# Later use of modulation weights and pinned first activations in a two-layer diffusion trunk on one Trainium2 core

## The chip, the cores and the metric

The kernel runs on one core of a Trainium2 chip. The metric is device microseconds for one execution of the whole program, as the median of several runs. The engines are PE (TensorE, with its weight loads as PEld), DVE (VectorE), ACT (ScalarE), POOL (GpSimd) and SP (SyncE), whose queue issues most of the DMAs; ACT's queue issues the rest. Each engine works through its own instructions in the order in which they stand in its program.

## What is computed

The reference is one step of a two-layer trunk with 512 latent tokens and 128 context tokens, model width 1024, all in float32. Layer 0 mixes tokens with neighbourhood attention, layer 1 with grouped-query attention. Each is followed by a gated feed-forward block with a depthwise convolution of width 3. Every sub-layer is normed before and after, and scaled, shifted and gated by rows of a modulation vector. Cut to what matters here:

```python
sh_as, sc_as, g_as, sh_fs, sc_fs, g_fs = adaln(c, ada_w[l], ada_b[l])   # silu(c) @ (1024 x 6144) + b
...
u = h @ w_up                                   # 1024 -> 2 x 2816
u = conv3(u) * conv_w + conv_b                 # along the tokens
a, gt = jnp.split(u, 2, axis=-1)
y = (jax.nn.silu(a) * gt) @ w_down             # 2816 -> 1024
x = x + g_fs * rmsnorm(y, norm_ffn_post[l])
```

## The kernel before

**Split products.** A float32 operand is held as a rounded high part and the low rest (`wh`/`wl`, `ahi`/`alo`, `vh`/`vl`, `ah`/`al`). ACT casts the high part (L165 for weights read whole, L1107 for up-projection blocks, L1075 for activations), DVE or POOL subtracts it to get the low part (L167, L1108, L1077). A product is then three matmuls per 128 rows.

**The up-projection.** The 5632 output columns are 22 pairs of blocks, one value block and one gate block of 128 columns each; a pair is called p. The first two pairs (`PLAIN`) run as plain products; the other 20 use a seven-product scheme in which sums of weight blocks (DVE, L1128 to L1131) meet sums of activation blocks. Inside the loop over p the seven products come in the order 6, 5, 1 (of the next pair), 7, 2 (of the next pair), 3, 4, each of 12 matmuls of 322 columns, into three banks `ux`, `uy`, `uz`. After each product its result is evicted: `c`, `u` and `v` are copies on ACT (L1161), `C` are sums on DVE (L1203, L1210, L1212) or a copy on ACT (L1216). A complete `C` goes through the convolution: `t` on ACT (L1182), two taps on DVE (L1184), then `sl` on ACT and `act` on DVE, and SP stores `act` of that pair to DRAM (L1223). `fetch` (L1099) loads the weights of later pairs into four buffers.

**Modulation weights.** `ada_work` is a generator. Each step of the loop of products calls `next(ada)` once. It loads 128x1024 pieces of `ada_w` (tile `wr`, three buffers, L275), uses three at a time in small matmuls (`ada`, L114), adds a bias (`arow`, L297) and writes a row of modulation values to DRAM (`modrow`, from ACT's queue). Layer 0's up-projection carries 48 such pieces (six rows of the next steps), layer 1's carries 8. The first layer's attention stage also calls it with steps = 1.

**The down-projection.** `load_dn(k, c0, c1)` loads one 128-row block of `w_down` (L163 in a helper) and the activations of pair k from DRAM (`ain`, three buffers, L1073), casts them to `ahi` (ACT, L1075, four buffers) and subtracts to `alo` (DVE, L1077). Two of these calls are written inside the last pair of the up-projection, the others after it. The token columns are handled in two ranges, 0 to 383 first (c0 = 0).

**The end of the mixer.** `Mix.second` runs the second half of the output projection tile by tile. During tile t it issues `fin.turns(t - 2)` (transposes to PSUM `tr`, ACT copies), `fin.residual(t - 1)` (DVE L377 and L386, ACT L348), and `low()`, which is the DVE subtraction of the low part of the transposed tile (`B<-tr,B`, L220). The first product of the up-projection reads that low part.

**What sets the order.** PE's order is exactly as written: a helper chains each matmul to the one before. On the other engines and on SP's queue a scheduler picks at build time, from what has its inputs and a free buffer, so an instruction may stand far ahead of the place where it was written. `tc.keep_in_program_order` holds an instruction to its written place. In the kernel before the scheduler put the first seven loads of `ain`, and the first four casts `ahi` and subtractions `alo`, into the first pairs of the up-projection, since `act` of pair k exists soon after pair k.

## Time and profile before

| | |
|---|---|
| median of 3 runs | 1622.42 us (1619.99 to 1624.73) |
| the profiled execution's own time | 1619.4 us |
| its span in the trace | 1617.6 us |
| mean granted TensorE clock | 0.984 |
| busy: PE, DVE, ACT, POOL | 1540.5, 1028.2, 860.7, 723.6 us |
| layer 0 up-projection (seven-product part) | about 427 to 705 us |
| layer 1 up-projection (seven-product part) | about 1198 to 1460 us |

The trace is one execution. A row of the timeline has start, duration, engine, line, operation, tiles, count and, in brackets, how long the engine sat idle before it and what ended that. Rows of the table of waits have the waiting instruction, what released it, the sum, the number and the longest.

### The profile page before, as it was taken

Reading aid. Unit: us, or ns where it says so; the run is one execution under the profiler, and the core shown is the slowest. Engines: PE = TensorE matmul, PEld = TensorE weight load, DVE = VectorE, ACT = ScalarE, POOL = GpSimd, SP = SyncE. Lnnn points to the kernel's source line nnn. Section 1 sums busy time; section 2 is a strip of 40 time slices with the busy share of each in tenths; the row PEclk is TensorE's granted clock in tenths of the full one; section 3 lists DMA queues with packets and bytes.
Section 4 is the critical chain, followed back from the end, with each engine's and each line's share of the span. In section 5 each row is a group of like instructions: output and inputs, shape, how many; then the busy total and the mean of one; then the engine's idle time right before and its main releaser. Section 6 shows DMA issues by size and latency. Waiting matters only on the chain.

```text
span 1617.6 us, 26048 instructions
## 1 busy us (share of the span) xinstructions
PE 1540.5 (95%) x9709; PEld 1357.0 (84%) x9709; DVE 1028.2 (64%) x1646; ACT 860.7 (53%) x1641; POOL 723.6 (45%) x613
## 2 busy tenths in 40 slices
PE   5999999899999999999999898999999999999998
PEld 3889899778988999998887667778889899998886
DVE  3453533539787666865656867774887887875554
ACT  3474655545555555654453536764555666564433
POOL 1554554324335555534444344441424556562433
PEclk8999999999999999999999998999999999999999
DMA  9745454236467764368574110004644333338664
GB/s 288 185 111 145 118 149 117 61 118 195 144 217 243 233 214 150 112 206 296 170 240 135 59 40 14 2 1 157 195 134 142 118 103 112 115 115 283 208 208 141
DMA packets 193211, 242.42 MB, mean 150 GB/s; under 512 B 11100, under 2 KB 149564, under 8 KB 193084
## 3 DMA queue, kind: packets, MB, share of 16 engines
q1 hardware_dynamic: 182224, 233.13, 45.2%
q10 hardware_dynamic: 10860, 7.62, 2.7%
q8 instruction: 76, 1.25, 0.3%
q14 instruction: 51, 0.42, 0.1%
HBM read 214.38 MB, written 26.34 MB: 149 GB/s over the span
## 4 chain that ended last, share of the span: by engine, by line
PE 65%; DVE 11%; POOL 8%; issue 6%; DMA 5%; ACT 3%; SPq 1%; ACTq 1%; POOLq 0%; DVEq 0%
PE acc L114 18%; PE ux L114 11%; PE y L114 7%; PE qk L114 5%; PE uz L114 4%; PE po L114 4%; PE s L114 3%; PE uy L114 3%; PE vp L114 3%; PE tp L117 3%; POOL wl L1108 3%; PE ada L114 2%; POOL vl L1108 2%; DMA wr<-in_ada_w 2%; DVE t L1184 1%
## 5 line engine op out<-in xcount | busy, mean ns | idle before, releaser
L167 POOL TENSOR_TENSOR wl<-wr,wh 128x1024 fp32r<-128x1024 f32 x74 | 181.3, 2453 | 257.9 <-ACT wh L165 249.8
L1108 POOL TENSOR_TENSOR wl<-wr,wh 128x1024 fp32r<-128x1024 f32 x80 | 193.9, 2446 | 36.9 <-ACT wh L1107 29.9
L114 PE MATMUL ux<-B,wh 128*128 128x322 f32 x832 | 201.2, 313 | 2.2 <-DVE B L220 1.6
L1184 DVE SCALAR_TENSOR_TENSOR t<-C,cw,t 128x644 f32<-128x644 f32 x176 | 156.3, 888 | 51.8 <-ACT t L1182 51.2
L114 PE MATMUL acc<-wh,alo 128*128 128x512 f32 x440 | 172.0, 391 | 0.0
L114 PE MATMUL acc<-wh,ahi 128*128 128x512 f32 x440 | 171.9, 391 | 0.0
L114 PE MATMUL acc<-wl,ahi 128*128 128x512 f32 x440 | 171.8, 390 | 0.0
L165 ACT CAST wh<-wr 128x1024 fp32r<-128x1024 f32 x140 | 145.4, 1048 | 37.5 <-DMA wr<-in_ffn_w_down 26.8
L114 PE MATMUL uz<-B,wh 128*128 128x322 f32 x640 | 156.5, 312 | 1.4 <-ACT v L1161 1.4
L114 PEld LDWEIGHTS ux<-B,wh 128*128 128x128 f32 x832 | 144.0, 189 | 5.5 <-DVE B L220 2.2
L1077 DVE TENSOR_TENSOR alo<-ain,ahi 128x384 fp32r<-128x384 f32 (+1 forms) x88 | 79.0, 910 | 92.7 <-ACT ahi L1075 92.3
L114 PE MATMUL ux<-B,wl 128*128 128x322 f32 x416 | 129.3, 311 | 0.0
L114 PE MATMUL qk<-hT,wh 128*128 128x384 f32 (+1 forms) x512 | 123.0, 317 | 0.1
L1108 POOL TENSOR_TENSOR vl<-wr,vh 128x1024 fp32r<-128x1024 f32 x38 | 99.5, 2619 | 40.8 <-ACT vh L1107 40.6
L114 PEld LDWEIGHTS uz<-B,wh 128*128 128x128 f32 x640 | 110.9, 188 | 4.1 <-ACT v L1161 1.6
L1107 ACT CAST wh<-wr 128x1024 fp32r<-128x1024 f32 x88 | 88.8, 1049 | 36.2 <-DVE wr L1131 34.8
L1075 ACT CAST ahi<-ain 128x384 fp32r<-128x384 f32 (+1 forms) x88 | 40.1, 460 | 120.6 <-PE acc L114 90.5
L167 DVE TENSOR_TENSOR wl<-wr,wh 128x1024 fp32r<-128x1024 f32 x66 | 84.8, 1297 | 26.5 <-ACT wh L165 26.0
L1182 ACT ACTIVATE t<-C,cw 128x644 f32<-128x644 f32 x88 | 78.6, 893 | 42.5 <-DVE C L1212 35.7
L114 PE MATMUL uz<-B,wl 128*128 128x322 f32 x320 | 99.5, 311 | 0.0
L114 PEld LDWEIGHTS acc<-wl,ahi 128*128 128x128 f32 x440 | 82.6, 188 | 17.9
L114 PEld LDWEIGHTS acc<-wh,alo 128*128 128x128 f32 x440 | 82.6, 188 | 17.8
(249 smaller groups left out, 4008.9 us busy)
## 6 DMA issues: line engine op xcount, KB each, us to landing
wr<-in_ffn_w_up SPq DMA_DIRECT2D x88, 512.0 KB
wr<-in_ffn_w_down SPq DMA_DIRECT2D x88, 512.0 KB
wr<-in_ada_w SPq DMA_DIRECT2D x80, 512.0 KB
act<-act SPq DMA_DIRECT2D x44, 321.0 KB
wr<-in_na_w_qkv SPq DMA_DIRECT2D x24, 512.0 KB
mod<-modrow SPq DMA_DIRECT2D x20, 512.0 KB
ain<-act SPq DMA_DIRECT2D x44, 192.0 KB
wf<-in_ada_w SPq DMA_DIRECT2D x16, 512.0 KB
```

What stands on the lines that cost most here:

```text
L114: pe(nc.tensor.matmul(*a, **k))
L117: pe(nc.tensor.transpose(*a, **k))
L165: i = nc.scalar.copy(hi, raw)
L167: j = (low or nc.vector).tensor_sub(lo, raw, f32(hi))
L1075: nc.scalar.copy(hi[:, 0 : c1 - c0], ain[:, 0 : c1 - c0])
L1077: nc.vector.tensor_sub(lo[:, 0 : c1 - c0], ain[:, 0 : c1 - c0], f32(hi[:, 0 : c1 - c0]))
L1107: nc.scalar.copy(hl[0], src)
L1108: low.tensor_sub(hl[1], src, f32(hl[0]))
L1182: nc.scalar.activation(t, taps(0), AF.Identity, bias=cw[:, 3, n : n + 1], scale=cw[:, 1, n : n + 1])
L1184: nc.vector.scalar_tensor_tensor(t, taps(d), cw[:, w, n : n + 1], t, op0=ALU.mult, op1=ALU.add)
```

## The change

It has three parts. (1) In the two up-projections the generator of modulation weights yields four times, not once, between its first three loads and their use, and a group is used every eight products instead of six; the three loads of the next group are written in the first three of the eight steps. For steps = 1 nothing changes. (2) In `Mix.second`, for the last tile alone, `low()` is written before `fin.residual(t - 1)` instead of behind it. (3) For k < 4 of the first token range, the load `ain`, the cast `ahi` and the subtraction `alo` are held in program order.

```diff
-    def ada_work(p, rawp, group, steps, todo):
+    def ada_work(p, rawp, group, steps, todo, wait=1):
...
         for _ in range(group):
             load()
-        yield
+        for _ in range(wait):
+            yield
         while raws:
...
             for i in range(steps):
-                for _ in range(n * i // steps, n * (i + 1) // steps):
+                for _ in range(n if steps == 1 else i < n):
                     load()
                 yield
...
                         low = fin.turns(t - 2) if t >= 2 else None
+                        if low and t == NT - 1:
+                            low()
                         if t >= 1:
                             fin.residual(t - 1)
-                        if low:
+                        if low and t < NT - 1:
                             low()
...
         def load_dn(k, c0, c1, own=None):
+            pin = tc.keep_in_program_order if k < 4 and c0 == 0 else lambda i: i
...
-            nc.sync.dma_start(ain[:, 0 : c1 - c0], actd[k][:, c0:c1])
+            pin(nc.sync.dma_start(ain[:, 0 : c1 - c0], actd[k][:, c0:c1]))
...
-            nc.scalar.copy(hi[:, 0 : c1 - c0], ain[:, 0 : c1 - c0])
+            pin(nc.scalar.copy(hi[:, 0 : c1 - c0], ain[:, 0 : c1 - c0]))
...
-            nc.vector.tensor_sub(lo[:, 0 : c1 - c0], ain[:, 0 : c1 - c0], f32(hi[:, 0 : c1 - c0]))
+            pin(nc.vector.tensor_sub(lo[:, 0 : c1 - c0], ain[:, 0 : c1 - c0], f32(hi[:, 0 : c1 - c0])))
...
-                ada = ada_work(adap, s2.enter_context(pool("adar", 3, side)), 3, 6, todo)
+                ada = ada_work(adap, s2.enter_context(pool("adar", 3, side)), 3, 8, todo, 4)
```

Layer 0's 48 pieces make 16 groups of three: before, the last was used behind product 92 of 138, now behind 125. On PE the first group of a layer stands behind five products instead of two.

The first place is SP's queue at the start of layer 1's up-projection. `act_k` is the DRAM tensor of pair k, `wr<-in_ffn_w_up` the weights of later pairs. Before:

```order
L275 DMA wr<-in_ada_w 128x1024
L1073 DMA ain<-act_0_12441 128x384
L275 DMA wr<-in_ada_w 128x1024 x2
L1223 DMA act_1_12442<-act 128x642
L1073 DMA ain<-act_1_12442 128x384
L1099 DMA wr<-in_ffn_w_up 128x8x128 x2
L1223 DMA act_2_12443<-act 128x642
L1073 DMA ain<-act_2_12443 128x384
```

and after, from the store of pair 0:

```order
L1227 DMA act_0_12441<-act 128x642
L275 DMA wr<-in_ada_w 128x1024 x2
L1227 DMA act_1_12442<-act 128x642
L1103 DMA wr<-in_ffn_w_up 128x8x128 x2
L275 DMA wr<-in_ada_w 128x1024 x2
L1227 DMA act_2_12443<-act 128x642
```

The loads of `ain` are gone from this place; they stand in the last two pairs now.

The second place is ACT in the same pairs. Before:

```order
L1161 COPY u_13064<-ux 128x322
L1075 CAST ahi<-ain 128x384
L1161 COPY v_13091<-uz 128x322
L1182 ACTIVATE t<-C,cw_84 128x2x322
L1161 COPY c_13112<-ux 128x322
L1107 CAST wh<-wr 128x1024 x2
```

and after:

```order
L1165 COPY u_13064<-ux 128x322
L1165 COPY v_13079<-uz 128x322
L1165 COPY c_13098<-ux 128x322
L1186 ACTIVATE t<-C,cw_84 128x2x322
L1111 CAST wh<-wr 128x1024 x2
```

The cast of `ahi`, which stood between the eviction copies `u` and `v`, is no longer there.

The third place is ACT in the last two pairs of layer 1's up-projection, where the first casts for the down-projection (L165) stand. Before:

```order
L165 CAST wh<-wr 128x1024 x2
L1182 ACTIVATE t<-C,cw_84 128x2x322
L1216 COPY C<-ux 128x322
L1161 COPY u_15525<-ux 128x322
L1190 ACTIVATE sl<-t 128x644
L1182 ACTIVATE t<-C,cw_84 128x2x322
L1161 COPY v_15540<-uz 128x322
```

and after:

```order
L165 CAST wh<-wr 128x1024
L1079 CAST ahi<-ain 128x384
L165 CAST wh<-wr 128x1024
L1186 ACTIVATE t<-C,cw_84 128x2x322
L1220 COPY C<-ux 128x322
L1079 CAST ahi<-ain 128x384
L1165 COPY u_15525<-ux 128x322
L1194 ACTIVATE sl<-t 128x644
L1186 ACTIVATE t<-C,cw_84 128x2x322
L1165 COPY v_15540<-uz 128x322
```

Two casts of `ahi` stand now ahead of the copies `u` and `v` of the last pair, and two more behind them. On DVE the first `alo` stands there directly ahead of the sum `C<-uz` of the pair before.

## Prediction

> **What bounds the kernel now.** I read the page's first lines, then the busy time of the two up-projections, then PE's waits in each.

> ```profile
> span 1617.6 us, 26048 instructions
> PE 1540.5 (95%) x9709; PEld 1357.0 (84%) x9709; DVE 1028.2 (64%) x1646; ACT 860.7 (53%) x1641; POOL 723.6 (45%) x613
> ```

> PE is busy for 95% of the span. Its work is not changed by a single matmul, so the change can only win PE's idle time or lengthen it. The windows of layer 1's and layer 0's up-projections say how much there is (duration, then busy PE, PEld, DVE, ACT, POOL, granted clock, DMA share, GB/s):

> ```profile
> 1160.00:1460.00 300.00, 288.56 (x1953) 281.26 (x1952) 244.79 (x308) 177.21 (x261) 153.02 (x91) 1.00 0.40 126
> 395.00:705.00 310.00, 302.44 (x2228) 284.23 (x2227) 225.30 (x307) 172.95 (x254) 147.37 (x86) 0.99 0.57 185
> ```

> PE idles 7.6 us of layer 0's 310 and 11.4 us of layer 1's 300. DVE, the next busiest, has 82% in layer 1 and 73% in layer 0: near, not at the bound. What PE waited for, layer 0 first, then layer 1:

> ```profile
> PE ada L114 <- DMA wr<-in_ada_w: 4.0, 5, 1.6
> PE uy L114 <- DVE C L1232: 2.6, 1, 2.6
> PE ux L114 <- ACT u L1161: 0.5, 1, 0.5
> PE ux L114 <- POOL vl L1108: 0.4, 1, 0.4
> ```

> ```profile
> PE ada L114 <- DMA wr<-in_ada_w: 2.8, 3, 1.5
> PE uy L114 <- DVE C L1232: 2.6, 1, 2.6
> PE ux L114 <- POOL vl L1108: 1.6, 4, 0.7
> PE ux L114 <- DVE C L1210: 1.5, 1, 1.5
> PE uz L114 <- ACT v L1161: 1.4, 1, 1.4
> PE ux L114 <- DVE B L220: 0.8, 1, 0.8
> ```

> The first row of each is part 1 of the change; ACT `u`, ACT `v`, DVE `C` and some of POOL `vl` will turn out to be part 3; DVE `B L220` is part 2.

> **Part 1, the modulation weights.** PE at the first group of layer 0, a later group, and the queue's issue of that later group:

> ```profile
> 430.36 0.64 PE L114 MATMUL ada<-wr,scolp 128*32 128x256 f32 x8
> 432.61 0.64 PE L114 MATMUL ada<-wr,scolp 128*32 128x256 f32 x8 [1.61 <-DMA wr<-in_ada_w]
> 433.87 0.64 PE L114 MATMUL ada<-wr,scolp 128*32 128x256 f32 x8 [0.62 <-DMA wr<-in_ada_w]
> ...
> 497.28 0.64 PE L114 MATMUL ada<-wr,scolp 128*32 128x256 f32 x8 [0.59 <-DMA wr<-in_ada_w]
> ...
> 489.55 1.47 SPq L275 DMA_DIRECT2D wr<-in_ada_w  x3
> ```

> The first group finds its third piece 433.87 - 430.36 = 3.5 us late. It moves back by three products. A pair of seven products takes 12.46 us (row below), so a product is 1.78 us and the delay 5.3 us: enough. A later group is short by about 0.6 us on its third piece; the interval grows by two products, 3.6 us: also enough. So 4.0 + 2.8 = 6.8 us of shown waits go, eight of them. Each costs more than it shows, since the matmuls before and behind it no longer overlap; from the rows of part 3 I take 0.28 us for each, 2.2 us in all. Part 1: -9.0 us. The matmuls themselves stay. They now run to product 125 of 138, and the pieces come every eight products instead of six; PE fills that time anyway and the DMA engines were at 57% with the denser loads, so I cost the move at nothing. Without that cover it would cost a wait of some 0.6 us at a group again. On SP the loads still stand between stores of `act` and loads of `w_up`; ends for part 1 are 0, if the queue holds them back as long as before, and -9.0.

> **Part 3, where the casts leave.** The queue, ACT and PE at the second hoisted activation of layer 1, and two ACT casts `ah` of the undisturbed stretch:

> ```profile
> 1243.30 0.53 SPq L1223 DMA_DIRECT2D act<-act  x1
> 1248.78 0.32 SPq L1073 DMA_DIRECT2D ain<-act  x1
> ```

> ```profile
> 1243.79 0.62 ACT L1107 CAST ah<-wr 128x512 fp32r<-128x512 f32 x1 [0.36 <-PE ux L114]
> 1252.40 0.51 ACT L1075 CAST ahi<-ain 128x384 fp32r<-128x384 f32 x1 [6.41 <-DMA ain<-act]
> 1254.39 0.42 ACT L1161 COPY v<-uz 128x322 f32<-128x322 f32 x1
> 1260.53 0.62 ACT L1107 CAST ah<-wr 128x512 fp32r<-128x512 f32 x1 [0.43 <-PE ux L114]
> ...
> 1426.35 0.62 ACT L1107 CAST ah<-wr 128x512 fp32r<-128x512 f32 x1 [0.36 <-PE ux L114]
> 1438.81 0.62 ACT L1107 CAST ah<-wr 128x512 fp32r<-128x512 f32 x1 [0.36 <-PE ux L114]
> ```

> ```profile
> 1248.02 0.42 PE L114 MATMUL ux<-B,vl 128*128 128x322 f32 x1 [0.55 <-POOL vl L1108]
> ```

> SP issues `ain` only when the store of the same pair has landed, 5.5 us after that store. ACT then stands 6.41 us at `ahi`, and the copy `v` queued behind it is late; PE waits 1.4 us for `v` and 1.5 us for the `C` that needs it. A pair takes 1438.81 - 1426.35 = 12.46 us where nothing waits, this one 1260.53 - 1243.79 = 16.74: 4.28 us more, against shown waits of 0.55 + 1.4 + 1.5 = 3.4 in three places. That is the 0.28 us per wait used above. What goes: layer 1's `v` and `C` (2.9), the two longest of `vl` (0.55 and 0.7), layer 0's `u` (0.5): 4.65 us shown and 5 x 0.28: -6.1 us. The short rest of the `vl` waits I leave as it is.

> **Part 3, where the casts arrive.** The last two pairs of layer 1, on ACT, DVE, POOL, SP and PE; and a slow `alo` from before:

> ```profile
> 1448.01 1.04 ACT L165 CAST wh<-wr 128x1024 fp32r<-128x1024 f32 x1
> ...
> 1451.57 0.89 ACT L1182 ACTIVATE t<-C,cw 128x644 f32<-128x644 f32 x1 [0.57 <-DVE C L1212]
> ...
> 1455.92 0.42 ACT L1161 COPY v<-uz 128x322 f32<-128x322 f32 x1
> ```

> ```profile
> 1229.93 2.05 DVE L1077 TENSOR_TENSOR alo<-ain,ahi 128x384 fp32r<-128x384 f32 x1
> ...
> 1451.05 0.48 DVE L1212 TENSOR_TENSOR C<-uz,u 128x322 f32<-128x322 f32 x1
> ```

> ```profile
> 1447.23 5.77 POOL L1108 TENSOR_TENSOR wl<-wr,wh 128x1024 fp32r<-128x1024 f32 x2 [4.63 <-ACT wh L1107]
> ```

> ```profile
> 1437.45 2.69 SPq L163 DMA_DIRECT2D wr<-in_ffn_w_down  x2
> ```

> ```profile
> 1456.87 0.31 PE L114 MATMUL uz<-B,wh 128*128 128x322 f32 x1
> ```

> The first `alo` now stands ahead of `C<-uz` on DVE. ACT's `t` waits for that `C`, and `u`, `sl`, `t` and `v` are queued behind it. PE's product 3 accumulates in the bank that `v` copies, and starts at 1456.87, 0.53 us after `v` ends (1455.92 + 0.42). So a delay x costs x - 0.53 plus the 0.28. An `alo` of up to 0.53 us, about what its cast took on ACT (0.51), would cost nothing; beside a busy POOL it took 2.05 us, and POOL is in its two `wl` here. I take the latter: 1.8 us for each layer, +3.6 us; ends 0 and +3.6. The cast in ACT fits the idle time around it. `ain` for k = 0 is issued right behind the first `w_down`, so about 10 us before ACT reaches it (1437.45 to 1448.01); a lone load landed in 3.6 us (1248.78 to 1252.40). `ahi` for k = 2 and 3 is first needed behind the first two blocks of the down-projection, whose `w_down` casts are in time today.

> [...]

> **Part 2, the low half of the last tile.** DVE before the first product, and the two windows of the long wait, layer 0 and layer 1:

> ```profile
> 387.08 1.28 DVE L386 TENSOR_TENSOR xm<-xo,mod 128x512 f32<-128x512 f32 x2
> 388.29 0.76 DVE L220 TENSOR_TENSOR B<-tr,B 128x264 fp32r<-128x264 f32 x2
> ```

> ```profile
> 398.00:405.00 7.00, 4.43 (x20) 4.17 (x19) 6.93 (x10) 4.75 (x8) 0.15 (x4) 0.76 0.30 91
> 1171.00:1178.00 7.00, 4.43 (x30) 4.17 (x29) 7.00 (x10) 4.01 (x8) 0.13 (x2) 1.00 0.30 85
> ```

> One `B<-tr,B` passes one of the two L386, so PE's 0.8 us wait shrinks by some 0.6 us. But PE then waits 2.6 us for DVE's `C` L1232, and DVE is busy for all 7 us there; the same instructions in another order end at the same time. PE only arrives earlier at a longer wait: 0. Ends: -1.2 us for both layers if DVE follows, +1.7 us if the clock does (below).

> **Sum.** -9.0 - 6.1 + 3.6 + 0 = -11.5 us. The profiled execution took 1619.4 us, 3.0 below the median of the runs; taken from 1619.4 it gives 1607.9, from the median 1622.42 it gives 1610.9. I predict a median of 1611.

> **Rivals.** (a) The chain of DVE, ACT and POOL takes over in layer 1, so that PE's early gain is only waited away at `vl`. For it: DVE's 82%, and the four `vl` waits. Against: layer 0, where `ada` matmuls slow PE, shows a single one. It would take back part 1's share of layer 1, 2.8 + 3 x 0.28 = 3.6 us: 1614.5. (b) The loads stay late, since SP holds them behind stores: only part 3 is left, -2.5 us: 1619.9, no change. Against it: 489.55 to 497.28 is 7.7 us, and the need was 0.6 us. (c) Slower: the pinned casts wait for `ain` as they did before, now in the last pairs, where `w_down` is on the same queue. Each such wait costs 4.28 us by the pair above; with four of the eight the sum turns to +5.6 us, 1628, and from three on nothing is won. It needs a landing later than 10 us. (d) The clock: layer 0's window was granted 0.76, layer 1's 1.00, after the same 2.6 us wait. With PE's wait grown to 3.2 us, layer 1 could be halved too. A loss of 0.24 of 7 us is 1.7 us: 1612.6. [...]

> **How the numbers follow.** Forecast 0.58, (a) 0.16, (d) 0.10, (b) 0.10, (c) 0.06. About 0.3%, 4.9 us, is what a measurement of this kernel can tell from no change, so faster is below 1617.6: the forecast, (d) and most of (a), 0.81. Same: (b) and the slow end of (a), 0.13. Slower: 0.06. Range: low 1604, where the arrival costs nothing (-3.6) and DVE follows PE in part 2 or layer 0 keeps its clock (-1.2 to -1.7), rounded for the spread of the runs; high 1619, which leaves out (c) and most of (b).

> **What the profile after would show.** No PE wait for `in_ada_w` in either up-projection; if some stay, the lead is too short. No ACT wait for `ain` near the start; pairs of 12.46 us plus the `ada` matmuls there. PE waits of about 1.5 us at `uz` or `ux` in the last pair, on ACT `v` or `u`; none means the arrival was free. The waits at `B L220` shorter and those at `C L1232` longer by the same. Wrong would be: ACT waiting for `ain` in the last pairs, or `vl` waits that grow from 2.0 us by as much as the `ada` waits fall.

## The result, and the profile after

The changed kernel took 1611.22 us (1610.03 to 1611.9, four runs), the kernel before 1621.2 us beside it (1619.02 to 1624.73, four runs): ratio 0.9941, 95% interval 0.9922 to 0.9959. The forecast was 1611. The total came out; several of its terms did not, as the experiments show.

The page of the changed kernel, first lines:

```profile
span 1608.2 us, 26065 instructions
PE 1541.6 (96%) x9709; PEld 1360.4 (85%) x9709; DVE 1023.0 (64%) x1646; ACT 860.6 (54%) x1641; POOL 722.2 (45%) x613
```

PE does the same 9709 matmuls in 1541.6 us (1540.5 before); the span is 9.4 us shorter. What PE waits for after the change, layer 0 (395 to 705 us) and then layer 1 (1150 to 1460 us):

```profile
PE uy L114 <- DVE C L1236: 3.2, 1, 3.2
PE acc L114 <- DVE alo L1081: 0.2, 1, 0.2
```

```profile
PE uy L114 <- DVE C L1236: 3.2, 1, 3.2
PE ux L114 <- ACT u L1165: 0.9, 1, 0.9
PE ux L114 <- POOL vl L1112: 0.9, 4, 0.3
PE uz L114 <- ACT v L1165: 0.7, 1, 0.7
PE acc L114 <- DVE alo L1081: 0.3, 1, 0.3
PE ux L114 <- DVE B L220: 0.2, 1, 0.2
```

The rows for `in_ada_w` are gone from both layers (4.0 and 2.8 us before), and so are `u` in layer 0 and the waits of 1.4 us for `v` and 1.5 us for `C` in layer 1. New are `u` and `v` at the end of layer 1 and `alo` at the first product of the down-projection. `B L220` fell from 0.8 to 0.2, and the wait for `C` behind it rose from 2.6 to 3.2.

A pair of landmarks per layer measures the stretch between: PE's `uy` behind the long wait for `C`, and the first `acc`. Before, and after:

```profile
401.07 0.42 PE L114 MATMUL uy<-B,wh 128*128 128x322 f32 x1 [2.56 <-DVE C L1232]
705.31 0.39 PE L114 MATMUL acc<-wh,ahi 128*128 128x512 f32 x1
1173.96 0.41 PE L114 MATMUL uy<-B,wh 128*128 128x322 f32 x1 [2.57 <-DVE C L1232]
1460.42 0.40 PE L114 MATMUL acc<-wh,ahi 128*128 128x512 f32 x1
```

```profile
401.16 0.42 PE L114 MATMUL uy<-B,wh 128*128 128x322 f32 x1 [3.18 <-DVE C L1236]
698.74 0.40 PE L114 MATMUL acc<-wh,ahi 128*128 128x512 f32 x1
1168.51 0.42 PE L114 MATMUL uy<-B,wh 128*128 128x322 f32 x1 [3.18 <-DVE C L1236]
1450.43 0.40 PE L114 MATMUL acc<-wh,ahi 128*128 128x512 f32 x1
```

Layer 0 went from 705.31 - 401.07 = 304.24 to 297.58 us (-6.7), layer 1 from 286.46 to 281.92 us (-4.5). The prediction had about -4.4 and -7.1. Everything outside the two stretches grew by 1.8 us together, which gives the 9.4 us of the span; 0.6 of it lies behind layer 1's first `acc`, and the rest is not followed up here. Layer 1 lost part of its share at its start, where PE's granted clock was 0.50 behind the longer wait (windows of the changed kernel; the seventh value is the granted clock):

```profile
1166.40:1169.80 3.40, 1.29 (x8) 1.29 (x9) 3.40 (x5) 1.67 (x3) 0.13 (x2) 1.00 0.08 22
1169.80:1173.20 3.40, 3.40 (x15) 3.40 (x14) 3.40 (x6) 0.83 (x1) 0.00 (x0) 0.50 0.48 137
```

PE is busy for the whole 3.40 us of the second row at a granted clock of 0.50: by that share 1.7 us lost, an estimate. The profiled execution of the kernel before did not lose it here; it was granted 1.00 from 1169.58 to 1176.41 us, around the same wait.

### The profile page after: what moved, and what is told of

Same layout as the page of the kernel before. It is cut to its first block, busy times and chain, and to the rows that moved or that the text cites. A ratio compares the mean times of both kernels' runs of the same rounds, so it can differ in the third digit from the quotient of the medians.

```text
span 1608.2 us, 26065 instructions
## 1 busy us (share of the span) xinstructions
PE 1541.6 (96%) x9709; PEld 1360.4 (85%) x9709; DVE 1023.0 (64%) x1646; ACT 860.6 (54%) x1641; POOL 722.2 (45%) x613
## 4 chain that ended last, share of the span: by engine, by line
PE 73%; DVE 10%; POOL 6%; issue 4%; ACT 4%; DMA 2%; SPq 1%; ACTq 0%; POOLq 0%; DVEq 0%
PE acc L114 18%; PE ux L114 15%; PE y L114 7%; PE uz L114 6%; PE qk L114 5%; PE uy L114 4%; PE po L114 4%; PE s L114 4%; PE vp L114 3%; PE tp L117 3%; PE ada L114 2%; POOL wl L1112 1%; DVE al L1112 1%; POOL vl L1112 1%; DMA wf<-in_ada_w 1%
## 5 line engine op out<-in xcount | busy, mean ns | idle before, releaser
L114 PE MATMUL ux<-B,wh 128*128 128x322 f32 x832 | 201.9, 314 | 1.4 <-ACT u L1165 0.9
L114 PE MATMUL acc<-wh,alo 128*128 128x512 f32 x440 | 172.3, 392 | 0.6 <-DVE alo L1081 0.6
L114 PE MATMUL acc<-wh,ahi 128*128 128x512 f32 x440 | 171.9, 391 | 0.0
L114 PE MATMUL acc<-wl,ahi 128*128 128x512 f32 x440 | 171.9, 391 | 0.0
L165 ACT CAST wh<-wr 128x1024 fp32r<-128x1024 f32 x140 | 145.5, 1048 | 33.5 <-DMA wr<-in_ffn_w_down 24.3
L114 PE MATMUL uz<-B,wh 128*128 128x322 f32 x640 | 156.5, 313 | 0.7 <-ACT v L1165 0.7
L114 PEld LDWEIGHTS ux<-B,wh 128*128 128x128 f32 x832 | 145.0, 190 | 4.3 <-ACT u L1165 1.2
L114 PE MATMUL ux<-B,wl 128*128 128x322 f32 x416 | 130.1, 313 | 0.2
L114 PE MATMUL qk<-hT,wh 128*128 128x384 f32 (+1 forms) x512 | 122.8, 317 | 0.1
L114 PEld LDWEIGHTS uz<-B,wh 128*128 128x128 f32 x640 | 110.9, 188 | 3.6 <-ACT vh L1111 1.6
L114 PE MATMUL uz<-B,wl 128*128 128x322 f32 x320 | 99.5, 311 | 0.1
L114 PEld LDWEIGHTS acc<-wh,alo 128*128 128x128 f32 x440 | 82.5, 188 | 19.1 <-DVE alo L1081 1.4
L114 PEld LDWEIGHTS acc<-wl,ahi 128*128 128x128 f32 x440 | 82.6, 188 | 17.8
```

Source lines behind the costliest of these rows:

```text
L114: pe(nc.tensor.matmul(*a, **k))
L165: i = nc.scalar.copy(hi, raw)
```

## Experiments

Twelve kernels ran in three groups of four, each against the kernel before on the same chip. Times are medians; the difference to before is of medians in the same group. The ratio and its interval are not formed from these two medians and can differ from them: for the interval of eight alone the medians give -3.5 us, the ratio -1.9 us.

| kernel | time, us | against before, us | ratio (95%) |
|---|---|---|---|
| part 1 alone | 1606.53 | -14.2 | 0.9912 (0.9897 to 0.9926) |
| part 3 alone | 1620.08 | -0.6 | 0.9995 (0.9986 to 1.0004) |
| part 2 alone | 1621.16 | +0.5 | 1.0007 (0.9997 to 1.0018) |
| parts 1 and 3 | 1608.65 | -12.1 | 0.9918 (0.9905 to 0.9932) |
| before, one cast moved in layer 1 | 1617.54 | -2.1 | 0.9990 (0.9979 to 1.0001) |
| part 1, one cast moved in layer 0 | 1604.66 | -15.0 | 0.9914 (0.9899 to 0.9928) |
| lead of four alone | 1622.04 | +2.4 | 1.0021 (1.0011 to 1.0031) |
| interval of eight alone | 1616.10 | -3.5 | 0.9988 (0.9978 to 0.9998) |
| part 1 in layer 1 | 1610.70 | -9.1 | 0.9941 (0.9927 to 0.9955) |
| part 1 in layer 0 | 1614.59 | -5.2 | 0.9965 (0.9952 to 0.9979) |
| lead of four and part 3 | 1621.70 | +1.9 | 1.0005 (0.9994 to 1.0016) |
| parts 1 and 3, `alo` later | 1606.42 | -13.4 | 0.9915 (0.9901 to 0.9929) |

### Part 1 alone

```diff
-        yield
+        for _ in range(wait):
+            yield
...
-                for _ in range(n * i // steps, n * (i + 1) // steps):
+                for _ in range(n if steps == 1 else i < n):
...
-                ada = ada_work(adap, s2.enter_context(pool("adar", 3, side)), 3, 6, todo)
+                ada = ada_work(adap, s2.enter_context(pool("adar", 3, side)), 3, 8, todo, 4)
```

> The kernel before with part 1 alone (lead of four products, a group every eight, loads in the first three steps). Theory T, the terms of the prediction add up: the eight waits for in_ada_w go, -9.0 us, of which 5.4 in layer 0 (4.0 shown + 5 x 0.28) and 3.6 in layer 1 (2.8 + 3 x 0.28). Rival (a), the chain of DVE, ACT and POOL takes layer 1's share back: -5.4 us, and the PE waits at vl in layer 1 grow from 1.6 to some 4 us. Rival (b), the loads stay late on SP's queue: 0.

Measured: -14.2 us, beyond every theory. The same landmarks, and PE's waits in layer 1:

```profile
401.69 0.42 PE L114 MATMUL uy<-B,wh 128*128 128x322 f32 x1 [2.59 <-DVE C L1233]
700.46 0.39 PE L114 MATMUL acc<-wh,ahi 128*128 128x512 f32 x1
1168.08 0.41 PE L114 MATMUL uy<-B,wh 128*128 128x322 f32 x1 [2.58 <-DVE C L1233]
1447.54 0.40 PE L114 MATMUL acc<-wh,ahi 128*128 128x512 f32 x1
```

```profile
PE uy L114 <- DVE C L1233: 2.6, 1, 2.6
PE ux L114 <- POOL vl L1109: 2.2, 8, 0.6
PE ux L114 <- DVE B L220: 0.8, 1, 0.8
```

Layer 0 is 298.77 us long: -5.5, where -5.4 was expected. Layer 1 is 279.46: -7.0 instead of -3.6. The waits for `v` and `C` are gone there too, though the casts `ahi` are still in the early pairs. ACT at the fourth of them shows why:

```profile
1238.65 0.42 ACT L1162 COPY u<-ux 128x322 f32<-128x322 f32 x1
...
1240.38 0.43 ACT L1162 COPY v<-uz 128x322 f32<-128x322 f32 x1 [0.52 <-PE ux L114]
1240.70 0.52 ACT L1076 CAST ahi<-ain 128x384 fp32r<-128x384 f32 x1
```

In the kernel before this cast stood between `u` and `v` and held `v` up for 6.41 us of waiting; here the build-time order, chosen anew around the moved loads, has it behind `v`, with its input there. So what I had booked under part 3 was already won by part 1. The time fell by more than the two stretches, 14.2 against 12.5 us; the runs with part 1 in one layer take this up.

### Part 3 alone

```diff
+            pin = tc.keep_in_program_order if k < 4 and c0 == 0 else lambda i: i
...
+            pin(nc.sync.dma_start(ain[:, 0 : c1 - c0], actd[k][:, c0:c1]))
...
+            pin(nc.scalar.copy(hi[:, 0 : c1 - c0], ain[:, 0 : c1 - c0]))
...
+            pin(nc.vector.tensor_sub(lo[:, 0 : c1 - c0], ain[:, 0 : c1 - c0], f32(hi[:, 0 : c1 - c0])))
```

> The kernel before with part 3 alone (loads, casts and subtractions of the first four activations held in their written place). T: -6.1 us at the start of the two layers and +3.6 us at their ends, -2.5 us in all. If the arrival costs layer 1 alone, as the trace after suggests (waits of 0.95 and 0.72 for u and v in layer 1, none in layer 0, where the last group of modulation weights leaves PE behind): about -4 us. If it costs nothing: -6.1 us. Here layer 0 has no late group of weights before the last pair (its last stands behind product 92), so T expects the waits for u and v in layer 0 too, and the sum of -2.5.

Measured: no difference. The early waits went, and the late ones came in both layers (`u` 0.65 and `v` 0.74 in layer 0, 0.94 and 0.75 in layer 1, and 0.25 and 0.23 for `alo` a few us behind the first `acc`). But the first group of weights of layer 1 waits for 3.7 us here (2.8 before), and the clock follows:

```profile
1203.40:1206.80 3.40, 0.96 (x16) 0.32 (x16) 1.78 (x2) 3.34 (x5) 2.65 (x2) 1.00 0.86 293
1206.80:1210.20 3.40, 2.94 (x21) 1.63 (x14) 1.79 (x2) 0.18 (x1) 0.10 (x1) 0.50 1.00 308
1210.20:1213.60 3.40, 3.40 (x15) 3.40 (x14) 0.00 (x0) 0.43 (x1) 0.00 (x0) 0.50 0.86 242
```

PE idles for 2.44 us of the first window and is granted 0.50 in the next two, by that share a loss of up to 3.4 us. Layer 0's first group waited 3.0 us in this execution (2.2 before) and had a half clock of 3.4 us behind it too, another 1.7 us by the same estimate. Its two stretches are 1.3 and 1.0 us longer than those of before, though the early waits are gone. So the trace shows the early waits leaving, and it does not show what part 3 is worth by itself.

### Part 2 alone

```diff
+                        if low and t == NT - 1:
+                            low()
                         if t >= 1:
                             fin.residual(t - 1)
-                        if low:
+                        if low and t < NT - 1:
                             low()
```

> The kernel before with part 2 alone (low half of the last tile earlier). T: the wait at B L220 shrinks by 0.6 us in each layer and the wait at C L1232 grows by as much, from 2.57 to 3.18 us; 0 us. Rival (d), the longer wait halves the clock in layer 1 as in layer 0: +1.7 us, and layer 1's clock drops right behind that wait. If the change of the clock in layer 1 after was chance, layer 1 is not halved here.

Measured: no difference. `B L220` went to 0.2 and `C` to 3.2 us, as expected, but layer 1's clock stayed full behind that wait:

```profile
1168.80:1172.20 3.40, 1.87 (x13) 1.62 (x12) 2.31 (x5) 3.37 (x8) 1.89 (x4) 1.00 0.70 247
1172.20:1175.60 3.40, 1.74 (x12) 1.74 (x13) 3.40 (x6) 1.25 (x2) 0.13 (x2) 1.00 0.24 67
1175.60:1179.00 3.40, 3.40 (x26) 3.40 (x25) 3.40 (x6) 1.78 (x3) 0.00 (x0) 1.00 0.31 92
```

The wait ran from 1170.68 to 1173.87, so a boundary of the clock's windows (of 3.413 us, last section) split it into 1.5 and 1.7 us. In the changed kernel 2.15 us of a wait of the same length fell into one window, and the next was granted 0.50. So the longer wait alone did not bring a half clock here; the two executions differ in where it fell in the windows.

### Parts 1 and 3, without part 2

The changed kernel with the edit of part 2 undone.

> The changed kernel without part 2 (parts 1 and 3 on the kernel before). T with part 2 at zero: as the changed kernel, about -10 us against before. Rival (d), the 3.18 us wait is what halves layer 1's clock: this kernel keeps 2.57 us there, layer 1 stays at full clock, and it is 1.7 us faster than the changed kernel, about -12 us against before.

Measured: -12.1 us, layer 1 at full clock behind the wait of 2.57 us. Its layer 1 took 280.12 us, 1.8 less than in the changed kernel, about the 1.7 us estimated for its window at 0.50. As times, its ratio and that of the changed kernel overlap, so what part 2 costs there is shown by the two traces alone. Beside part 1 alone (same group) it is 2.1 us slower by the medians, with overlapping intervals: on top of part 1, part 3 gained nothing that can be measured.

### One cast moved

On the kernel before, and on part 1 alone, an order was added: `ahi` of each of the first four activations behind the copy `v` of its pair. In the built order this moves one cast and its `alo` in each kernel: in layer 1 of the one, in layer 0 of the other. In the first, SP also issues one load of `w_up` apart from its partner.

```diff
-            nc.scalar.copy(hi[:, 0 : c1 - c0], ain[:, 0 : c1 - c0])
+            i = nc.scalar.copy(hi[:, 0 : c1 - c0], ain[:, 0 : c1 - c0])
+            if k < 4 and c0 == 0:
+                tc.add_manual_dep(i.ins, vcopy[k + 2].ins.name, no_sync, reason="order")
...
-                nc.scalar.copy(small[name, p], u)
+                i = nc.scalar.copy(small[name, p], u)
+                if name == "v5":
+                    vcopy[p] = i
```

> The kernel before, and one thing moved: in layer 1 the fourth early cast ahi (and its subtraction alo) stands behind the copy v of its pair on ACT, instead of between u and v; the other seven early casts stay where they are, and so do the modulation weights. Theory P (what costs is the place among the eviction copies where the build-time order puts a late cast, not that the cast stands in the early pairs): the waits for v (1.36), for C (1.52) and most of the two vl waits around them go, the pair of 16.74 us becomes one of about 12.5 to 13, so -3.5 to -4.3 us. Theory Q (the early loads and casts themselves cost, through SP's queue, as part 3 assumes): the waits only move to c or to the next u, 0 to -1 us.

> Part 1 alone, and one thing moved: in layer 0 the fourth early cast ahi (and its alo) stands behind the copies u and v of its pair instead of ahead of u. Theory P: the one wait for u that part 1 alone still has there (1.14 us) goes, -1.1 to -1.4 us against part 1 alone, so about -15 us against before; no other wait appears. Theory Q: the wait turns up at c or v, no change against part 1 alone.

On the kernel before: -2.1 us by the medians, the interval just reaching no change. The trace is clearer. ACT at the moved cast:

```profile
1254.60 0.42 ACT L1164 COPY v<-uz 128x322 f32<-128x322 f32 x1
1256.19 0.52 ACT L1076 CAST ahi<-ain 128x384 fp32r<-128x384 f32 x1 [1.18 <-DMA ain<-act]
1256.61 0.42 ACT L1164 COPY c<-ux 128x322 f32<-128x322 f32 x1
```

The cast still waits for its input, and nobody waits for it: PE has no wait for `v` or `C` there, and the pair between two casts `ah` of ACT takes 12.47 (1248.62 to 1261.09) instead of 16.74 us. P holds for the waits, Q does not. The time of this execution does not show it: it is the longest of the twelve, its first group of layer 1 waited 4.1 us and the clock was then halved for 6.8 us, so its layer 1 takes 286.41 us, as before (286.46). That the median fell by 2.1 us and not by 3.5 or more is not explained by this one trace.

On part 1: 1604.66 us, the lowest median of all. The wait of 1.14 us for `u` is gone and layer 0 has one wait left:

```profile
PE uy L114 <- DVE C L1238: 2.3, 1, 2.3
```

The interval does not separate this kernel from part 1 alone; its layer 0 is 297.66 us against 298.77, -1.1 as expected. That stretch is steady: with the same order in layer 0, part 1 in layer 0 alone (below) took 298.81. Layer 1 is less so: it is 1.3 us shorter here (278.12 against 279.46) though nothing was moved in it.

### The two halves of part 1, and one of them with part 3

The first `+` line is one kernel and the second another; the loop over `wait` is as in part 1. The third kernel is the first one with part 3.

```diff
-                ada = ada_work(adap, s2.enter_context(pool("adar", 3, side)), 3, 6, todo)
+                ada = ada_work(adap, s2.enter_context(pool("adar", 3, side)), 3, 6, todo, 4)   # lead alone, loads spread as before
+                ada = ada_work(adap, s2.enter_context(pool("adar", 3, side)), 3, 8, todo, 1)   # interval alone, loads in the first three steps
```

> The kernel before with the first half of part 1: the generator yields four times before the first group, but a group is still used every six products with its loads spread over the six. T: the waits of the first group in each layer go (2.2 in layer 0, 2.8 in layer 1), the 0.6 us at some later groups of layer 0 stay: -5.0 - 6 x 0.28 = -6.7 us at most. P: the fourth early cast of layer 1 stands ahead of the copy u of its pair here, and the third ahead of u or v, so the waits of some 3 us for u, v and C in that pair stay, whatever the modulation weights do.

> The kernel before with the other half of part 1: a group every eight products, loads in the first three steps, but the first group two products after its loads as before. T: the first group's waits stay (2.2 in layer 0, 2.8 in layer 1), the three of 0.6 us at later groups of layer 0 go: -1.8 - 3 x 0.28 = -2.6 us. P: the fourth early cast of layer 1 stands ahead of the copy u of its pair here too, so its waits of some 3 us stay.

> The lead of four products with the old interval of six and the old spread of loads, and part 3. Without part 3 this lead made the kernel no faster: its trace shows a load of ain that stands 7 us on SP's queue, waiting for the store of its pair, ahead of a load of in_ada_w, and then a PE wait of 4.07 us for in_ada_w. Theory S (the early ain loads on SP's queue are what makes the weights late): with the ain loads moved to the end, the waits of 4.07, 2.76 and 1.23 go and the kernel is about as fast as with parts 1 and 3, -9 to -12 us against before. Theory D (the spread of loads over six steps is too tight by itself): waits of 1 us and more for in_ada_w stay in layer 0, -2 to -5 us.

The lead alone made the kernel slower (+2.4 us) where T had -6.7: the first group is in time, but layer 0 now waits 8.5 us at later ones, and behind the wait of 4.1 us the clock is halved for 6.8 us.

```profile
PE ada L114 <- DMA wr<-in_ada_w: 8.5, 5, 4.1
```

The interval alone gave -3.5 us by the medians and -1.9 by the ratio, around T's -2.6: the first groups still wait. P holds in both traces for the place: early casts in layer 1 stand ahead of `u` or `v`, and PE waits for `C` 1.06 and `u` 0.47 us in the one, for `u` twice 1.18 us in the other. These waits are smaller than the 3 us that P named.

The third kernel tests whether the early `ain` loads on SP's queue make the weights late. It had none there and was no faster than before. PE's waits in its layer 0, and SP's queue:

```profile
PE ada L114 <- DMA wr<-in_ada_w: 6.6, 4, 3.7
```

```profile
461.90 0.33 SPq L275 DMA_DIRECT2D wr<-in_ada_w  x1
...
468.76 9.33 SPq L275 DMA_DIRECT2D wr<-in_ada_w  x5
```

So S falls. One piece of the group that PE uses at 475 us is issued at 461.90, the other two not before 468.76, behind loads of `w_up`, of a bias and a gain, and a store of `act`: loads written late in an interval of six come late. D expected waits of this kind, though its -2 to -5 us did not come either: behind the waits the clock is halved for 3.4 us twice, and layer 0 takes 310.83 us (304.24 before). Whether the eight steps or the loads written in the first three of them matter more was not separated; of the versions here, only those with both and the lead have every group in time.

### Part 1 in one layer at a time

```diff
-                for _ in range(n * i // steps, n * (i + 1) // steps):
+                for _ in range(n * i // steps, n * (i + 1) // steps) if steps < 8 else range(i < n):
...
-                ada = ada_work(adap, s2.enter_context(pool("adar", 3, side)), 3, 6, todo)
+                every, lead = (8, 4) if l == 1 else (6, 1)    # and with l == 0
+                ada = ada_work(adap, s2.enter_context(pool("adar", 3, side)), 3, every, todo, lead)
```

> Part 1 in layer 1 alone; layer 0 keeps the lead of one step and the interval of six. T, with the terms of the prediction: -3.6 us (2.8 of waits + 3 x 0.28). P: the build-time order now puts the fourth early cast of layer 1 behind v, so the waits for v and C and the long vl go as well, some -3.5 more. K (clock): in four of five profiles whose first group of layer 1 waits some 3 us for its weights, the clock is halved for 3.4 to 6.8 us right behind, 1.7 to 3.4 us; with part 1 that goes too. P and K together: -7 to -10 us, and more than half of what part 1 gives in both layers.

> Part 1 in layer 0 alone; layer 1 stays as before, its fourth early cast still ahead of v. T: -5.4 us. P and K add nothing here, since layer 0's waits were short and no half clock follows them: -5.4 as well, and this run and the one for layer 1 add up to part 1's -14. If they do not add up, the layers are coupled through something else.

Measured: -9.1 and -5.2 us, together -14.3, the -14.2 of both. Layer 0 is as the prediction had it. Layer 1 is worth 9.1 instead of 3.6. Its stretch is 278.77 us, 7.7 less than in the trace of before: 5.7 us of shown waits (the three pieces of the first group, `v`, `C`) and 2 us of hidden ones. The rest, about 1.4 us, fits what K names: the first group of layer 1 waits 2.8 to 4.1 us in the profiles of the six kernels that keep the old lead there, and five of them (part 3, part 2, one cast moved, interval, part 1 in layer 0) have a half clock of 3.4 or 6.8 us right behind. The profiled execution of the kernel before is the sixth, without one: a boundary of the clock's windows, at 1203.71 us, split its wait into 1.5 and 1.3 us. I had read its price for that wait as the usual one. That the half clock makes up the rest is fitted to six profiles of six kernels; no run tried it by itself.

### The entry

```diff
+            if k == 0 and c0 == 0:
+                tc.add_manual_dep(i.ins, anchor[0].ins.name, no_sync, reason="order")   # alo behind two taps of pair 20
...
+                    anchor[0] = tap[0]
```

> Parts 1 and 3, and one thing moved: the first alo stands behind the sum C<-uz and two taps of the pair before on DVE, not ahead of them. E (the alo ahead of C is what makes u and v late in the last pair): the waits for u (0.62) and v (0.72) in layer 1 go, -1.3 - 2 x 0.28 = -1.9 us against parts 1 and 3 without this, and layer 0 does not change, as it has no such waits. If the cast ahi ahead of u on ACT is the cause instead, the waits stay. The wait of 0.3 us for alo at the first product of the down-projection may grow.

The built order moves that `alo` in both layers, and on SP's queue one load of `ain` to a later place; ACT's order stays as it was. PE's waits in layer 1 with parts 1 and 3, and with the `alo` moved:

```profile
PE uz L114 <- ACT v L1163: 0.7, 1, 0.7
PE ux L114 <- ACT u L1163: 0.6, 1, 0.6
...
PE acc L114 <- DVE alo L1079: 0.3, 1, 0.3
```

```profile
PE acc L114 <- DVE alo L1080: 1.3, 1, 1.3
```

E holds: both waits are gone with the casts on ACT left as they were, and layer 1 is 2.0 us shorter (278.14 against 280.12). Half of it is given back one step later, at `alo`. As times the two kernels are not separated (ratios 0.9918 and 0.9915).

## Why the prediction came out, and where it was wrong

The total was right by luck: errors of opposite sign met. Built up in steps, by the medians, part 1 gave -14.2 us, 5.2 more than its term of -9.0. Part 3 on top of it took the gain to -12.1, so it cost 2.1 where the sum had -2.5. Part 2 took it to -10.0 (the changed kernel, measured in another group), another 2.1 where the sum had 0. Neither of the last two steps is clear of the intervals, so their sizes are rough; that part 3 did not bring its 2.5 us a second time is what the terms below rest on.

**Part 1 (-9.0).** The mechanism was right and no wait for `in_ada_w` was left. Layer 0's term was right too: -5.2 measured against -5.4, and the hidden cost per wait held, since part 1 alone took 3.8 us of shown waits net out of layer 0 (4.0, `u` 0.5 and `vl` 0.4, less a new `u` of 1.1) and shortened it by 5.5, which is 0.28 us for each of six waits. Layer 1's -3.6 was mis-sized: -9.1. The failed step is "I cost the move at nothing". Moving the loads gave ACT another order at the fourth cast, which is shown. It also took away a wait that has a half clock behind it in five of the six profiles that keep it; that this is the rest of the 9.1 us is argued.

**Part 3 leaving (-6.1).** The waits went as forecast. But as a term of a sum it was counted twice: with part 1 most of them go without it, and moving one cast behind `v` is enough on the kernel before. Part 3 alone gave -0.6 us, and nothing measurable on top of part 1 (+2.1 by the medians).

**Part 3 arriving (+3.6).** Half right. The rows of the changed kernel at the end of layer 1:

```profile
1435.21 5.76 POOL L1112 TENSOR_TENSOR wl<-wr,wh 128x1024 fp32r<-128x1024 f32 x2 [6.03 <-ACT wh L1111]
...
1439.04 2.35 DVE L1081 TENSOR_TENSOR alo<-ain,ahi 128x384 fp32r<-128x384 f32 x1
...
1441.32 0.48 DVE L1216 TENSOR_TENSOR C<-uz,u 128x322 f32<-128x322 f32 x1
```

`alo` took 2.35 us beside POOL's `wl` (2.05 was taken), and PE waited 0.95 and 0.72 us behind it: 1.67 shown, 2.2 with 0.28 each. That it is the `alo` and not the cast on ACT is what the entry's run shows. In layer 0 an `alo` of 2.35 us stands in the same place, and it cost nothing before the first `acc`. The trace shows a group of modulation weights on PE in nearly every pair there, the last at 673.82 us, about two pairs before the end (pairs of 14.1 us, where part 3 alone has 12.46 in its last four and does have the waits); that this slack hides the entry fits both kernels, but was not tried by itself. What I had not listed is the wait for `alo` 3.6 us behind the first `acc`, 0.25 and 0.30 us. The first `alo` started within a `wl` of POOL and ended at 1441.39, 0.42 us behind the end of that `wl` (1435.21 + 5.76 = 1440.97); the slow `alo` of before ended 0.42 us behind a POOL subtraction as well (1229.93 + 2.05 = 1231.98 and 1231.56):

```profile
1229.18 2.38 POOL L1108 TENSOR_TENSOR vl<-wr,vh 128x1024 fp32r<-128x1024 f32 x1
```

In the traces of before and after, the 25 `alo` of this shape that began within a POOL subtraction took 2.05 to 2.75 us, and each ended 0.41 or 0.42 us behind the end of that subtraction; the other 63 took 0.54 to 0.56 us. By these rows the delay was what was left of the POOL subtraction.

**Part 2 (0).** The two waits moved as written, 0.81 to 0.21 and 2.56 to 3.18 us, and alone the part gave nothing that can be measured. Its upper end, +1.7 us through the clock in layer 1, is what the profiled execution of the changed kernel shows.

**Rivals.** (d) came true in that execution, but not as a rule: with part 2 alone a wait of the same length left the clock full. (a) did not: the `vl` waits fell from 1.6 to 0.9 us, and with part 1 alone, where they rose to 2.2, layer 1 was won all the same. Of (b) nothing is left, as no group is late, and of (c) nothing either: ACT stands idle before none of the eight pinned casts, and PE's rows at the ends are `u`, `v` and `alo`.

## What to carry to other kernels

Where a scheduler chooses the order at build time, waits read from one trace are not a sum of independent prices: build each part alone and look where the instructions stand that other waits hang on. Here a late input cost by what stood behind its consumer in the queue: moving that consumer three instructions down took the pair from 16.74 to 12.47 us, with the input still late. Lengthening a lead without the interval and the place of the loads made this kernel slower, and of the versions here part 1 with one cast moved (1604.66 us) has the lowest median. It and part 1 alone lie below the changed kernel by their medians (-15.0 and -14.2 us against -10.0); the intervals of the ratios just overlap.

## Of the hardware, not expected

Three short waits of which 2.13 us fall into one window had a half clock behind them (part 2 alone, first group of layer 1), and one wait of 3.19 us that a boundary splits in two had none (the same kernel, `C`). Where the windows lie differed from profile to profile in layer 1, where two of 14 long waits for `C` were followed by a half clock; in layer 0 it was all 14.
